# Four products of a pair summed in one PSUM bank, and fourteen more projections of the mixing stages computed as pairs

## The chip, the cores and the metric

The kernel runs on one core of one Trainium2 chip. The metric is the device time of one execution in microseconds. Every matmul works on float32 data split into a high and a low part (float32r), three matmuls for one product.

## The reference, cut to what matters

Two layers; each is an FFN, a mixing block with three branches, a second FFN and a gated embedding. All 544 tokens (512 of one prompt, 32 of eight samples) go through together. The mixing block is where most of the change lies:

```python
h = rmsnorm(x, w['g_mix'])
z = h @ w['w_in']
u_a, v_a, b_gate, c_gate, x_b, x_c, gates = jnp.split(z, SPLITS, axis=-1)
u_a = jax.nn.gelu(u_a)
v_a = layernorm(jax.nn.gelu(v_a), w['a_ln_g'], w['a_ln_b'])
y_a = chunk_spatial_gate(u_a, v_a, w['a_ws'], w['a_bs']) @ w['a_out']
conv_out, new_conv = short_conv(c_gate * x_b, conv_buf, w['b_conv'])
y_b = (b_gate * conv_out) @ w['b_out']
pooled, new_pool = multiscale_pool(x_c, pool_buf, start)     # windows 2, 4, 8, 16
y_c = (einsum(pooled, w['c_w']) * w['c_scale']) @ w['c_out']
g = jax.nn.sigmoid(gates)
x = x + (g[0] * y_a + g[1] * y_b + g[2] * y_c) @ w['w_o']
```

An FFN is `x + 0.5 * ((silu(gate) * up) @ w_down)` with `gate, up = split(rmsnorm(x) @ w_up)`.

## The kernel before

Activations stand with channels on the 128 partitions and the 544 tokens along the free axis, in slots of 128 x 544 float32 (85 slots in all, handed out in the order in which they came free). A weight block is 128 x 128; four blocks make a unit of 128 x 512, one DMA of 256 KB.

**Plain projections.** `gemm` (L302 is its matmul) multiplies one output block of 128 channels: 8 input blocks, three matmuls each, two halves of 272 tokens, so 48 matmuls of 272 columns, into a PSUM tile of two banks.

**Pairs.** `s_pair` computes two output blocks at once in the manner of Strassen and Winograd: seven products (`PRODUCTS`) of 12 matmuls of 272 columns each (L325 in `mm_s`), 84 matmuls where two plain projections have 96. Inputs B11, B21, B22 are halves of the input, T1 to T4 sums of halves; weights W12, W21, W22 are blocks, R1 to R4 sums of blocks. `ring_bank` hands out eight places of half a PSUM tile in turn; each product takes the next place, and ScalarE (L579) and VectorE (L581 to L593) add the seven results up in SBUF. FFN up-projections and the gates and U of the mixing block are pairs; C, XB, B and XC are plain; V is token-major (L807): tokens on the partitions, the normalized input as the stationary operand.

**Weights.** A planner lists all units in order. When TensorE's program reaches unit u, `unit` issues the low half of unit u+4 (L249, VectorE), the high half of u+5 (L244, ScalarE), the block sum of u+6 (L237, VectorE, for R3 and R4) and the loads of u+15 (SP's queue; for R1 and R2 a second load that accumulates, in POOL's queue). In plain stages `EXTRA` lets the low halves run up to 24 units ahead where slots allow.

**Order.** Every engine runs its instructions in program order, and the order is written out by hand. After each unit `tick` issues what is due: the `later` list (steps that follow a pair: SiLU, products, splits) and a share of the `background` list, such that it empties over a given number of ticks. `flush` issues all that is left at once.

**A mixing block**, in order: C0 and XB0 together, k outermost, with the rstd of the norm made beside them; then the background list of 24 steps that make the normalized input and the T sums of the pairs (`s_inputs` with `full`), over 24 ticks; convolution j (`conv_in`) after each of C/XB 1 to 3; V, its Gelu (L813) and its statistics (L814); B0 to B3; branch 1 (gate pairs and b_out); XC3 to XC0, each followed by its pooling (`pool_in`, `pool_mean`, `pool_out`); branch 2, where behind its first gate pair come the pool mixing (`c_mix`) and the first U pair; second U pair, spatial gate, branch 0, w_o.

Of the kernel before, what the change touches and what calls it, by code (L numbers as in the profile page):

```python
# [44 lines left out]
RMS_AT = 7, 14  # L45
RMS_AT0 = 8, 1
# [20 lines left out]
PRODUCTS = (("W21", "B11"), ("R3", "T2"), ("W22", "B21"), ("R1", "T1"), ("R2", "T3"), ("R4", "B22"), ("W12", "T4"))  # L67
# [35 lines left out]
class Kern:  # L103
# [217 lines left out]
    def mm_s(self, ps, w, xs, q, first, last):  # L321
        wh, wl = (a[:, q * P:(q + 1) * P] for a in w)
        xh, xl = xs
        for i, (a, b) in enumerate(((wl, xh), (wh, xh), (wh, xl))):
            self.nc.tensor.matmul(ps, a, b, start=first and i == 0, stop=last and i == 2)  # L325
# [77 lines left out]
    def s_inputs(self, gain, full):  # L403
# [5 lines left out]
        def steps(q):  # L409
# [45 lines left out]
            def sums():  # L455
                A, E = (e[0] for e in st["e"])
                st["t"] = self.slot()
                B = st["t"][0]
                nc.vector.tensor_sub(A[:, h1], A[:, h1], A[:, h2])
                nc.vector.tensor_sub(B[:, h2], A[:, h2], E[:, h2])  # L460
                nc.vector.tensor_add(B[:, h1], E[:, h2], A[:, h1])
                nc.vector.tensor_sub(A[:, h2], E[:, h1], B[:, h1])
                self.drop(st["e"][1])
# [103 lines left out]
    def s_pair(self, name, l, m1, m2, sets, s1, s2):  # L567
        nc = self.nc
        h1, h2 = slice(0, HT), slice(HT, T)
        q_ = self.slot()  # L570
        q1, V = q_[0][:, h1], q_[0][:, h2]
# [23 lines left out]
        self.drop(q_)  # L595

    def ff_group(self, up, l, j, inp, first, plain, hs, hsl):
# [47 lines left out]
        else:  # L645
            self.s_pair(up, l, NFF + j, j, inp.sets, o_, t_)
            d0()
# [59 lines left out]
    def to_seq(self, ps, buf, sbuf, lb, scale=True):  # L707
# [7 lines left out]
        for o, i, f in parts:  # L715
            if scale:
                nc.vector.tensor_mul(o, i, f)
            else:
                nc.scalar.activation(o, i, AF.Copy)
        return sv  # L720

    def mix(self, l, inp, nxt):
# [66 lines left out]
        assert len(xr) == KD  # L789
        self.drop(*xs)  # L790

# [6 lines left out]
        vslots = self.bank(3)  # L798
        vb = [vslots[i // 2][:, i % 2, :] for i in range(5)]
        self.extra = EXTRA[3]  # L800
        for k in range(KD):
            wh, wl = self.take("w_in", l, k, Z_V, 4)
            xh, xl = xr[k]
            for i in range(5):
                t0 = self.tok0(i)
                for q, (a, b) in enumerate(((xh, wl), (xh, wh), (xl, wh))):
                    nc.tensor.matmul(vb[i], a[:, t0:t0 + P], b, start=(k == 0 and q == 0), stop=(k == KD - 1 and q == 2))  # L807
# [4 lines left out]
        def v_in(i):  # L812
            nc.scalar.activation(vt[i][:, :SEQ], vb[i], AF.Gelu_apprx_tanh)  # L813
# [19 lines left out]

        for i in range(5):
            v_in(i)
        for j in range(G):
            pb, = self.gemm([W2(Z_B + j)])
            gate_b(j, pb)
# [433 lines left out]
```

## Time and profile before

| | us |
|---|---|
| median of 3 runs | 2437.67 (2436.99 to 2438.49) |
| span of the profiled execution, first to last instruction | 2435.3 |
| the rest of that median, outside the span | 2.4 |
| TensorE busy | 2414.3, 99% |
| VectorE busy | 1903.0, 78% |
| ScalarE busy | 1087.3, 45% |

The profile is of one execution. For that execution only the span is given; the times of the runs include what lies before the first and after the last instruction. A line such as L325 is a line of the kernel's file; a helper's line stands for all its callers. An entry "[2.50 <-PE ps L516]" says that the engine had stood idle for 2.50 us until TensorE's instruction of line 516 on tile ps was done.

### The profile page before, as it was taken

To read this page: it belongs to the slowest core of one execution; us is meant where nothing else is said; L and a number is where in the kernel's file an instruction comes from. 1 tells how busy PE (TensorE), PEld (TensorE's weight loads), DVE (VectorE), ACT (ScalarE), POOL (GpSimd) and SP (SyncE) were. 2 spreads that over 40 slices of the span, in tenths; PEclk is the share of its full clock that TensorE was granted. 3 is DMA by queue.
4 is the path that set the end of the run, shared out by engine and by line. 5 is a ranking of instruction groups with operands and counts; after the bars stand their busy time and mean duration, and the time that the engine had idled before them with its cause. 6 is when DMAs were issued, how large, how long until landed. Compare 5 with 4: busy or idle time off the path is not lost.

```text
span 2435.3 us, 48371 instructions
## 1 busy us (share of the span) xinstructions
PE 2414.3 (99%) x19016; PEld 2401.5 (99%) x19016; DVE 1903.0 (78%) x3583; ACT 1087.3 (45%) x2021; POOL 202.0 (8%) x248
## 2 busy tenths in 40 slices
PE   8999999999999999999999999999999999999997
PEld 8999999999999999999999999999999999999997
DVE  7887776778788887878788777866788779877775
ACT  6443444444446444435554444434354454434352
POOL 1111000010110100100010110000011011101000
PEclk9999999999999999999999999999999999999998
DMA  6665551354554555555255565523455536656521
GB/s 199 143 148 140 148 163 58 88 143 118 145 158 114 141 144 145 148 139 157 63 139 142 135 157 137 161 70 82 128 133 146 165 91 145 157 131 154 145 80 38
DMA packets 173988, 318.79 MB, mean 131 GB/s; under 512 B 19584, under 2 KB 21888, under 8 KB 173760
## 3 DMA queue, kind: packets, MB, share of 16 engines
q1 hardware_dynamic: 139248, 252.24, 34.2%
q0 software_dynamic: 32640, 61.16, 15.0%
q8 instruction: 149, 2.44, 0.4%
q10 hardware_dynamic: 1872, 2.29, 0.3%
q14 instruction: 79, 0.65, 0.1%
HBM read 312.63 MB, written 2.99 MB: 130 GB/s over the span
## 4 chain that ended last, share of the span: by engine, by line
PE 99%; DVE 0%; ACT 0%; DMA 0%; issue 0%; DVEq 0%; ACTq 0%
PE ps L325 47%; PE ps L302 46%; PE ps L807 2%; PE ps L1069 2%; PE ps L530 0%; PE ps L516 0%; PE ps L972 0%; DMA par<-in_par 0%; DVE s L1114 0%; PE ps L974 0%; DVE x L1096 0%; ACT s L1100 0%; ACT L502 0%; ACT L244 0%; DVE s L1095 0%
## 5 line engine op out<-in xcount | busy, mean ns | idle before, releaser
L325 PE MATMUL ps<-s,s 128*128 128x272 f32 x9156 | 1162.0, 288 | 0.0
L325 PEld LDWEIGHTS ps<-s,s 128*128 128x128 f32 x9156 | 1153.5, 188 | 0.4 <-DVE s L938 0.2
L302 PE MATMUL ps<-s,s 128*128 128x272 f32 x8880 | 1132.6, 288 | 7.3 <-ACT s L443 7.3
L302 PEld LDWEIGHTS ps<-s,s 128*128 128x128 f32 x8880 | 1121.7, 189 | 7.6 <-ACT s L443 7.2
L244 ACT ACTIVATE s<-s 128x512 fp32r<-128x512 f32 x1169 | 663.1, 621 | 506.0 <-DVE s L237 461.6
L249 DVE TENSOR_TENSOR s<-s,s 128x512 fp32r<-128x512 f32 x1169 | 768.3, 685 | 8.6 <-ACT s L244 8.6
L231 POOL DMA_DIRECT2D s<-in_wts x218 | 186.0, 854 | 1738.2 <-DMA s<-in_wts 448.5
L660 DVE SCALAR_TENSOR_TENSOR x<-ps,x 128x544 f32<-128x544 f32 x128 | 92.4, 722 | 137.2 <-PE ps L302 137.0
L579 ACT ACTIVATE s<-ps 128x272 f32<-128x272 f32 x109 | 43.2, 396 | 251.3 <-PE ps L325 251.1
L237 DVE TENSOR_TENSOR s<-s,s 128x512 f32<-128x512 f32 x218 | 149.3, 685 | 0.0
L581 DVE TENSOR_TENSOR s<-ps,s 128x272 f32<-128x272 f32 x109 | 48.0, 441 | 69.5 <-PE ps L325 43.3
L587 DVE TENSOR_TENSOR s<-ps,s 128x272 f32<-128x272 f32 x109 | 48.1, 441 | 63.8 <-PE ps L325 62.7
L607 ACT ACTIVATE s<-s 128x544 f32<-128x544 f32 x88 | 57.9, 658 | 89.4 <-DVE s L620 89.0
L613 ACT ACTIVATE s<-s 128x544 fp32r<-128x544 f32 x88 | 57.6, 654 | 59.8 <-DVE s L610 44.1
L864 DVE TENSOR_TENSOR s<-ps,s 128x544 f32<-128x544 f32 x48 | 34.8, 725 | 50.7 <-PE ps L302 46.2
L616 DVE TENSOR_TENSOR s<-s,s 128x544 fp32r<-128x544 f32 x88 | 63.2, 718 | 5.9 <-ACT s L613 5.8
L1069 PE MATMUL ps<-s,s 128*128 128x256 f32 (+1 forms) x480 | 61.6, 289 | 1.8 <-ACT rstd L532 1.8
L623 DVE TENSOR_TENSOR s<-s,rstd 128x544 f32<-128x544 f32 x88 | 63.2, 718 | 0.1
L1069 PEld LDWEIGHTS ps<-s,s 128*128 128x128 f32 x480 | 60.5, 188 | 2.0 <-ACT rstd L532 2.0
L610 DVE TENSOR_TENSOR s<-s,s 128x544 f32<-128x544 f32 x82 | 58.9, 718 | 0.4
L858 ACT ACTIVATE s<-s 128x544 f32<-128x544 f32 x48 | 29.0, 652 | 67.6 <-DVE s L593 67.6
L620 DVE TENSOR_TENSOR s<-s,rstd 128x544 f32<-128x544 f32 x82 | 59.0, 719 | 0.0
(133 smaller groups left out, 1176.4 us busy)
## 6 DMA issues: line engine op xcount, KB each, us to landing
s<-in_wts SPq DMA_DIRECT2D x951, 256.0 KB, 3.4
s<-in_wts POOLq DMA_DIRECT2D x218, 256.0 KB, 4.6
x<-in_xT ACTq DMA_DIRECT2D x4, 272.0 KB, 5.2
x<-in_xT SPq DMA_DIRECT2D x4, 272.0 KB, 4.8
s<-in_pT POOLq DMA_DIRECT2D x4, 272.0 KB, 3.2
out_yT<-s SPq DMA_DIRECT2D x4, 144.0 KB, 1.8
out_yT<-s ACTq DMA_DIRECT2D x4, 144.0 KB, 1.8
s<-in_st_in POOLq DMA_DIRECT2D x2, 272.0 KB, 3.1
```

Source lines behind the costliest of these rows:

```text
L231: self.nc.gpsimd.dma_start(out=t, in_=src(1 if w == "R1" else 2, 4), accum_op=ALU.add)
L237: self.nc.vector.tensor_add(self.new_raw(w, u0, 2 if w == "R3" else 1), self.read_raw(a, u0), self.read_raw(b, u0))
L244: self.nc.scalar.activation(a[0][:, :UC], self.read_raw(w, u0), AF.Copy)
L249: self.nc.vector.tensor_sub(lo, self.read_raw(w, u0), hi.bitcast(F32))
L302: self.nc.tensor.matmul(ps[:, h, :HT], a, bh, start=first and i == 0, stop=last and i == 2)
L325: self.nc.tensor.matmul(ps, a, b, start=first and i == 0, stop=last and i == 2)
L610: nc.vector.tensor_mul(o[:, :], o[:, :], t[:, :])
L616: nc.vector.tensor_sub(lo, o[:, :], hi.bitcast(F32))
L620: nc.vector.tensor_mul(t[:, :], t[:, :], self.rstd[:, :])
L623: nc.vector.tensor_mul(o[:, :], o[:, :], self.rstd[:, :])
L660: nc.vector.scalar_tensor_tensor(xm, self.pv(pst[i]), 0.5, xm, op0=ALU.mult, op1=ALU.add)
L1069: nc.tensor.matmul(ps, a, b[:, c], start=first and i == 0, stop=last and i == 2)
```

## The change

A pair takes four places of the ring, X, Y, Z and V, and skips one. The order of the products changes. R3, R1 and R4 go on accumulating in X on top of W21, with copies by ScalarE between them; the sign of T2 changes with it. The last evacuation can be given by the caller, so that rstd (FFN), the sigmoid (gates) or the Gelu (U) reads PSUM directly. In the mixing block V comes right after C0/XB0 and reads the input before normalization (rstd is then a scale of its Gelu, per token); the 24 input steps are spread over 9 ticks, the rest issued behind V; C/XB 1 to 3, B and XC become pairs, seven per layer. Pooling is cut into steps; the first U pair moves ahead of branch 2.

```diff
+V_TICKS = 9
-PRODUCTS = (("W21", "B11"), ("R3", "T2"), ("W22", "B21"), ("R1", "T1"), ("R2", "T3"), ("R4", "B22"), ("W12", "T4"))
+PRODUCTS = (("W21", "B11"), ("R2", "T3"), ("R3", "T2"), ("W22", "B21"), ("R1", "T1"), ("W12", "T4"), ("R4", "B22"))
...
+        X, Y, Z, V = (self.ring_bank()[:, :HT] for _ in range(4))
+        self.psi += 1
+        bank = {"W21": X, "R2": Y, "R3": X, "W22": Z, "R1": X, "W12": V, "R4": X}
         for i, (w, x) in enumerate(PRODUCTS):
-            bk = self.ring_bank()[:, :HT]
+            bk = bank[w]
             wt = self.s_unit(i, name, l, m1, m2)
+            new = w in ("W21", "R2", "W22", "W12")
             for q, xs in enumerate(sets):
-                self.mm_s(bk, wt, xs[x], q, q == 0, q == len(sets) - 1)
+                self.mm_s(bk, wt, xs[x], q, new and q == 0, q == len(sets) - 1, not new)
             if w == "W21":
-                nc.scalar.activation(q1, bk, AF.Copy)
+                nc.scalar.activation(b[:, h1], X, AF.Copy)
             elif w == "R3":
-                nc.vector.tensor_sub(V, bk, q1)
+                nc.scalar.activation(a[:, h2], X, AF.Copy)
+                nc.vector.tensor_sub(a[:, h1], Y, a[:, h2])
             elif w == "W22":
-                nc.vector.tensor_add(b[:, h1], bk, q1)
+                nc.vector.tensor_add(b[:, h1], Z, b[:, h1])
             elif w == "R1":
-                b5 = bk
-            elif w == "R2":
-                nc.vector.tensor_add(a[:, h1], bk, V)
-                nc.vector.tensor_sub(V, V, b5)
-                nc.vector.tensor_sub(a[:, h2], a[:, h1], b5)
+                nc.scalar.activation(b[:, h2], X, AF.Copy)
+                nc.vector.tensor_sub(a[:, h2], Y, b[:, h2])
+            elif w == "W12":
+                nc.vector.tensor_add(a[:, h1], V, a[:, h1])
             elif w == "R4":
-                nc.vector.tensor_sub(b[:, h2], bk, V)
-            else:
-                nc.vector.tensor_add(a[:, h1], a[:, h1], bk)
+                if last:
+                    last(b[:, h2], X)
+                else:
+                    nc.scalar.activation(b[:, h2], X, AF.Copy)
             self.tick()
...
         else:
-            self.s_pair(up, l, NFF + j, j, inp.sets, o_, t_)
-            d0()
+            r = self.rstd
+            self.s_pair(up, l, NFF + j, j, inp.sets, o_, t_,
+                        lambda out, ps: nc.vector.tensor_mul(out, ps, r[:, HT:]))
+            nc.vector.tensor_mul(t[:, :HT], t[:, :HT], r[:, :HT])
...
-        pc, px = self.gemm([W(Z_C), W(Z_XB)], kouter=True, hooks=self.rms_hooks(then=(steps, 24)))
+        pc, px = self.gemm([W(Z_C), W(Z_XB)], kouter=True, hooks=self.rms_hooks(then=(steps, V_TICKS)))
         conv_in(0, self.scaled(pc), conv_x(0, px))
-        for j in range(1, G):
-            pc1, = self.gemm([W(Z_C + j)])
-            c_ = self.scaled(pc1)
-            px1, = self.gemm([W(Z_XB + j)])
-            conv_in(j, c_, conv_x(j, px1))
...
-            nc.scalar.activation(vt[i][:, :SEQ], vb[i], AF.Gelu_apprx_tanh)
+            nc.scalar.activation(vt[i][:, :SEQ], vb[i], AF.Gelu_apprx_tanh, scale=self.cols[:, 16 + i:17 + i])
...
+        w = self.take("w_in", l, KD - 1, Z_V, 4)
         for i in range(5):
+            v_mm(KD - 1, w, i)
             v_in(i)
-        for j in range(G):
-            pb, = self.gemm([W2(Z_B + j)])
-            gate_b(j, pb)
+        while self.bg:
+            self.bg.popleft()()
+        self.drop(*xs)
+        for j in range(1, G):
+            c_, z_ = pair(Z_C + j, Z_XB + j)
+            conv_state(j)
+            conv_in(j, c_, self.slot(), z_)
+        for j in range(0, G, 2):
+            for i, b_ in enumerate(pair(Z_B + j, Z_B + j + 1)):
+                gate_b(j + i, b_)
...
-        for j in (3, 2, 1, 0):
-            st = {}
-            pj, = self.gemm([W2(Z_XC + j)])
-            pool_in(j, pj, st)
-            self.background([lambda j=j, st=st: pool_mean(j, st), lambda j=j, st=st: pool_out(j, st)], 3)
+        def pool_pair(j):
+            z1, z2 = pair(Z_XC + j, Z_XC + j + 1)
+            return pool_steps(j + 1, z2) + pool_steps(j, z1)
 
         self.flush()
+        self.background(pool_pair(2), 14)
+        fs = pool_pair(0)
+        self.flush()
+        self.background(fs, 12)
...
+        u_in(0)
 
         def c_mid():
+            self.flush()
             c_mix()
-            u_in(0)
```

`pool_steps` is a list: the input copies, one step per doubling of the window, the mean, and the split.

## Rows read from the trace of the kernel before

**Rows 1.** The page's first part: busy us (share of the span) xinstructions.

```profile
PE 2414.3 (99%) x19016; PEld 2401.5 (99%) x19016; DVE 1903.0 (78%) x3583; ACT 1087.3 (45%) x2021; POOL 202.0 (8%) x248
```

**Rows 2.** The chain that ended last, in order of time: start us, us, what.

```profile
433.12 27.75 PE ps L807 x120
460.87 24.05 PE ps L302 x192
484.91 10.52 PE ps L325 x84
```

**Rows 3.** Waits: engine, line, waited for, us in total, times, longest.

```profile
ACT s L579 <- PE ps L325: 251.1, 91, 5.5
...
PE ps L302 <- ACT s L443: 7.3, 1, 7.3
```

**Rows 4.** Groups by line: count, busy us, mean ns, idle before, releasers.

```profile
L249 DVE TENSOR_TENSOR s<-s,s 128x512 fp32r<-128x512 f32 x1169 | 768.3, 685 | 8.6 <-ACT s L244 8.6
L244 ACT ACTIVATE s<-s 128x512 fp32r<-128x512 f32 x1169 | 663.1, 621 | 506.0 <-DVE s L237 461.6 <-PE ps L302 31.7 <-PE ps L325 7.2
...
L587 DVE TENSOR_TENSOR s<-ps,s 128x272 f32<-128x272 f32 x109 | 48.1, 441 | 63.8 <-PE ps L325 62.7
...
L579 ACT ACTIVATE s<-ps 128x272 f32<-128x272 f32 x109 | 43.2, 396 | 251.3 <-PE ps L325 251.1
```

**Rows 5.** Timeline, first pair of an FFN: start us, us, instruction, count.

```profile
799.80 22.40 PE L325 MATMUL ps<-s,s 128*128 128x272 f32 x177
...
803.19 0.38 ACT L579 ACTIVATE s<-ps 128x272 f32<-128x272 f32 x1
```

**Rows 6.** Timeline, the pair behind the spatial gate.

```profile
671.01 10.77 PE L325 MATMUL ps<-s,s 128*128 128x272 f32 x84
...
674.04 0.38 ACT L579 ACTIVATE s<-ps 128x272 f32<-128x272 f32 x1
```

**Rows 7.** Timeline of VectorE behind V's statistics.

```profile
463.47 1.33 DVE L482 TENSOR_TENSOR s<-s,s 128x544 fp32r<-128x544 f32 x2
```

**Rows 8.** Timeline of VectorE and ScalarE at convolution 0 and during V.

```profile
397.87 0.69 DVE L748 TENSOR_TENSOR s<-s,s 128x512 f32<-128x512 f32 x1
...
399.44 0.31 ACT L760 ACTIVATE s<-cst,par 128x32 f32<-128x32 f32 x1
...
401.22 2.87 DVE L419 SCALAR_TENSOR_TENSOR s<-x,par,rstd 128x544 f32<-128x544 f32 x4
...
442.77 2.49 DVE L249 TENSOR_TENSOR s<-s,s 128x512 fp32r<-128x512 f32 x4
```

**Rows 9.** Timeline, pool 0 and the pair behind it.

```profile
574.95 10.67 PE L325 MATMUL ps<-s,s 128*128 128x272 f32 x84
575.15 0.76 ACT L719 ACTIVATE s<-ps 128x272 f32<-128x272 f32 x3 [1.64 <-PE ps L302]
...
575.84 0.71 DVE L907 TENSOR_TENSOR s<-s 128x526 f32<-128x526 f32 x1 [1.80 <-ACT s L719]
...
576.69 0.69 DVE L913 SCALAR_TENSOR_TENSOR s<-s,s 128x512 f32<-128x512 f32 x1
...
578.89 0.38 ACT L579 ACTIVATE s<-ps 128x272 f32<-128x272 f32 x1
```

**Rows 10.** Timeline of ScalarE at a change of its function table.

```profile
486.87 1.28 ACT L502 ACT_TABLE_LOAD   x1
488.17 0.21 ACT L502 ACTIVATE mv<-mv 128x5 f32<-128x5 f32 x1
```

**Rows 11.** Timeline, the pool mixing.

```profile
585.46 3.17 PE L302 MATMUL ps<-s,s 128*128 128x272 f32 x24
...
591.90 1.53 DVE L366 TENSOR_TENSOR s<-s,s 128x544 fp32r<-128x544 f32 x2
```

**Rows 12.** Stretches: busy us of PE, PEld, DVE, ACT, POOL; granted clock, DMA share, GB/s.

```profile
2400.00:2405.00 5.00, 3.24 (x25) 3.00 (x24) 3.64 (x9) 2.77 (x5) 0.00 (x0) 1.00 0.00 0
...
2420.00:2436.00 16.00, 3.29 (x15) 2.84 (x13) 7.42 (x23) 2.85 (x6) 0.00 (x0) 0.57 0.21 74
```

More of the change, by code (lines that the diff above doesn't have):

```diff
@@ L319, in gemm, with mm_s @@
         return pst
-    def mm_s(self, ps, w, xs, q, first, last):
+    def mm_s(self, ps, w, xs, q, first, last, go_on=False):
         wh, wl = (a[:, q * P:(q + 1) * P] for a in w)
@@ L324, in mm_s @@
         for i, (a, b) in enumerate(((wl, xh), (wh, xh), (wh, xl))):
-            self.nc.tensor.matmul(ps, a, b, start=first and i == 0, stop=last and i == 2)
+            self.nc.tensor.matmul(ps, a, b, start=first and i == 0, stop=last and i == 2, skip_group_check=go_on)
     def s_unit(self, i, name, l, m1, m2):
@@ L705, in nt, with to_seq @@
         return ap.rearrange("p (n t) -> p n t", t=t)
-    def to_seq(self, ps, buf, sbuf, lb, scale=True):
+    def to_seq(self, ps, buf, sbuf, lb):
         nc = self.nc
@@ L715, in to_seq @@
         for o, i, f in parts:
[L716 to L719, printed above, removed]
+            nc.vector.tensor_mul(o, i, f)
         return sv
@@ L797, in mix @@
         rows = [row("a_ln_g"), row("a_ln_b")]
-        vslots = self.bank(3)
+        vslots = [self.ps[(self.psi + i) % 4] for i in (0, 3, 1)]
+        self.psi += 2
         vb = [vslots[i // 2][:, i % 2, :] for i in range(5)]
         self.extra = EXTRA[3]
[L801 to L807, printed above, removed]
         vs = [self.slot() for _ in range(5)]
@@ L832, in v_bias, with v_mm @@
                 self.drop(rows[0], rows[1])
+        def v_mm(k, w, i):
+            wh, wl = w
+            xh, xl = xg[k]
+            t0 = self.tok0(i)
+            for q, (a, b) in enumerate(((xh, wl), (xh, wh), (xl, wh))):
+                nc.tensor.matmul(vb[i], a[:, t0:t0 + P], b, start=(k == 0 and q == 0), stop=(k == KD - 1 and q == 2))
+        for k in range(KD - 1):
+            w = self.take("w_in", l, k, Z_V, 4)
+            for i in range(5):
+                v_mm(k, w, i)
+        w = self.take("w_in", l, KD - 1, Z_V, 4)
         for i in range(5):
+            v_mm(KD - 1, w, i)
             v_in(i)
-        for j in range(G):
-            pb, = self.gemm([W2(Z_B + j)])
-            gate_b(j, pb)
+        while self.bg:
[3 more added lines that the diff above has]
+            c_, z_ = pair(Z_C + j, Z_XB + j)
+            conv_state(j)
+            conv_in(j, c_, self.slot(), z_)
+        for j in range(0, G, 2):
+            for i, b_ in enumerate(pair(Z_B + j, Z_B + j + 1)):
+                gate_b(j + i, b_)
         macc, merged, merged_s = [], [], []
@@ L855, in branch @@
             for m in range(0, KD, 2):
-                ts = pair(Z_G + br * KD + m, Z_G + br * KD + m + 1)
-                for t_ in ts:
-                    nc.scalar.activation(t_[0][:, :], t_[0][:, :], AF.Sigmoid)
+                ts = pair(Z_G + br * KD + m, Z_G + br * KD + m + 1, AF.Sigmoid)
                 if m == 0 and mid:
@@ L885, in mix, with pool_in @@
         po = st_po[0]
-        def pool_in(j, ps, st):
+        def pool_in(j, z_, st):
             st["sl"] = [self.slot() for _ in range(4)]
@@ L896, in pool_in, with pool_steps, begin, double @@
             nc.scalar.activation(self.nt(po[:, o:o + NS * LB], LB), sv[:, :, TS:], AF.Copy)
[L898 removed]
+        def pool_steps(j, z_):
             win = WINS[j]
[L900 to L906 removed]
+            st = {}
+            def begin():
+                pool_in(j, z_, st)
+                buf, ta, tb, sm = (t[0] for t in st["sl"])
+                st["cur"] = buf, sm[:, :QCOLS], 1
+                st["tmp"] = [(ta, sm[:, QCOLS:2 * QCOLS]), (tb, sm[:, 2 * QCOLS:3 * QCOLS])]
+            def double():
+                cur, scur, w = st["cur"]
+                nx, snx = st["tmp"][0]
+                st["tmp"].reverse()
@@ L915, in pool_mean @@
-            nc.vector.scalar_tensor_tensor(self.nt(out[:, SEQ:T], TS), cs[:, :, LB:], 1.0 / win,
-                                           st["sv"][:, :, LB:], op0=ALU.mult, op1=ALU.subtract)
-            h = win - 1
-            nc.vector.tensor_mul(out[:, :h], cur[:, LB:LB + h], self.par[:, PB_IC:PB_IC + h])
-            nc.vector.tensor_sub(out[:, :h], out[:, :h], buf[:, LB:LB + h])
-            st["o"] = next(t for t in st["sl"] if t[0] is out)
-            self.drop(*(t for t in st["sl"] if t is not st["o"]))
+                st["cur"] = nx, snx, 2 * w
@@ new lines, in mean @@
+            def mean():
+                cur, scur, _ = st["cur"]
+                buf, out = st["sl"][0][0], st["tmp"][0][0]
+                cs = self.nt(scur, LB + TS)
+                nc.vector.scalar_tensor_tensor(out[:, :SEQ], cur[:, LB:PCOLS], 1.0 / win, buf[:, LB:PCOLS],
+                                               op0=ALU.mult, op1=ALU.subtract)
+                nc.vector.scalar_tensor_tensor(self.nt(out[:, SEQ:T], TS), cs[:, :, LB:], 1.0 / win,
+                                               st["sv"][:, :, LB:], op0=ALU.mult, op1=ALU.subtract)
+                h = win - 1
+                nc.vector.tensor_mul(out[:, :h], cur[:, LB:LB + h], self.par[:, PB_IC:PB_IC + h])
+                nc.vector.tensor_sub(out[:, :h], out[:, :h], buf[:, LB:LB + h])
+                st["o"] = next(t for t in st["sl"] if t[0] is out)
+                self.drop(*(t for t in st["sl"] if t is not st["o"]))
@@ L923, in pool_out @@
+            return [begin] + [double] * (win.bit_length() - 1) + [mean, lambda: pool_out(j, st)]
         def pool_out(j, st):
```

67 lines of the change are left out of this document (27 added, 40 removed).

## The prediction

> **What bounds the kernel now.** I read the page's busy line first: TensorE is busy for 99% of the span, VectorE for 78, ScalarE for 45 [rows 1]. Then the chain in order of time, which is TensorE from end to end: a pair is 84 matmuls in 10.52 us, so a product 1.51, and a plain stretch of 192 matmuls takes 24.05 [rows 2]. Then the waits: TensorE's own view has four lines, the longest 7.3 us at the start (the others, 1.8 to 3.0 us, lie in the last stage) [rows 3]. Through all mixing and FFN stages TensorE waits for nothing. So a matmul taken away is time gained, a wait put in front of TensorE is time lost, both one for one, and the question is what waits the change makes.
>
> The groups by line give the other engines' prices [rows 4]: low half of a weight unit on VectorE 685 ns (L249; the weight sum, L237, is an addition of the same shape and taken alike), high half on ScalarE 621 (L244), a 272-column evacuation 396 on ScalarE (L579), 441 on VectorE (L587). Neighbours overlap: four L249 took 2.49 us, so they follow each other at (2.49 - 0.69)/3 = 0.60 us [rows 8]. With the same 0.085 off, I use 0.36 for short evacuations and 0.55 for a high half.
>
> **What goes.** Fourteen pairs replace 28 plain projections (per layer C/XB 1 to 3, two of B, two of XC). Two plain projections are 96 matmuls, half of 24.05; a pair saves 12.03 - 10.52 = 1.51 us [rows 2], fourteen **-21.1 us**. V keeps its 120 matmuls.
>
> **What comes: a deadline for ScalarE.** So far each product had a place of its own, read up to three products later. Now W21, R3, R1 and R4 add up in one place X, and TensorE may not start R3, R1 or R4 until ScalarE has copied X. One other product (R2, W22, W12) lies between, 1.51 us; a copy takes 0.40. So ScalarE may be about a microsecond late for nothing. It runs in order: ahead of a copy stand high halves, which wait for VectorE's sums, and background steps.
>
> *FFN pairs.* In 91 of 109 pairs ScalarE stood idle until W21 was done [rows 3], and VectorE gets less to do. For one back-to-back pair I count 9 weight operations at 0.60, 4 evacuations at 0.36, 0.7 for the rstd halves, 3 x 0.64 for the gate: 9.5 us of 10.5; the third copy, behind the sum for the next R3, ends 0.7 us early. Cost 0; with that cover gone, 0.1 us in each of 81 pairs is 8. The first pair of an FFN differs: its copy ran behind a flushed SiLU and split, 803.19 to 803.57; the pair began at 799.80, so R3 would be due at 802.81 [rows 5]. 0.76 late, three times: **+2.3**. Behind the spatial gate the copy ended at 674.42, R3 is due at 671.01 + 3.01 [rows 6]: 0.4, in two layers **+0.8**.
>
> *V to the first pair.* The 24 input steps go out over 9 ticks, but V has 8 units: 21 go out beside it, the last three (one high split, two low splits of T) stand in VectorE's queue behind V's five statistics. V's last matmul is at 433.12 + 27.75 = 460.87 [rows 2]; the statistics end at 463.47, two low splits take 1.33 [rows 7], the next two 1.27 more: done 5.2 us after V. The second product, R2 x T3, wants the last of them at 1.51 + 11/12 x 1.51 = 2.9. With a tenth of latency 2.4 us per layer, **+4.8**. Ahead of that VectorE has convolution 0 (4.8 with its evacuations) and 21 steps: 8 x 0.70 [rows 8], 12 x 0.64, 16 x 0.36, 19 us, against V's 27.75. So it reaches the statistics in time; some two us are left, and each weight half above three adds 0.6. Bounds per layer 1.5 to 5.
>
> *Pairs behind a convolution, three per layer.* Convolution j must now wait for ScalarE's copy of R4. In the old one VectorE was free 3.35 us after its first product (397.87 to 401.22), ScalarE 1.8 after it (399.44 + 0.31, less overlap) [rows 8]. From a pair's end: 0.5 + 1.8, a high half 0.55, the copy 0.4 = 3.25 against 3.01. VectorE, free at 3.85, makes a low half and a sum (5.05), ScalarE two high halves (6.2) and the next copy (6.6) against 6.3. 0.3 + 0.35 = 0.65 us, six times: **+3.9**. Bounds 0 to 8.
>
> *Pooling, the large one.* So far four plain projections of 6 us carried one pool each. Now pool 3 (four doublings) goes out in the second XC pair, and a flush sets all of pool 2 ahead of the next pair (U). The old kernel shows this in small, with pool 0 (one doubling) flushed ahead of a pair that began at 574.95: ScalarE's input copy at 575.15, a doubling at 575.84, the mean from 576.69, then split and high half, and the W21 copy from 578.89 to 579.27 [rows 9]. R3 would be due at 577.96: 1.31 late. Two things come on top. VectorE has in the second XC pair 8 x 0.60 + 4 x 0.36 + 4 x 0.85 + 1.1 up to pool 3's mean, and some 1.6 of waits for ScalarE: 12.3, so the mean ends 1.8 to 1.9 after the pair, its split takes 0.55, and pool 2's copy starts 2.25 later than pool 0's. And pool 2 has two doublings more, 1.7. 1.31 + 2.25 + 1.7 = 5.2 us per layer, **+10.4**. Bounds 3 (VectorE on time) to 7.
>
> Pools 1 and 0 then run beside that U pair and the gate pair behind it. U's third copy is 0.4 late. At U's end ScalarE has pool 1's split, a high half, the Gelu table (1.28 [rows 10]), three Gelus (1.35), a high half and the copy: if the table starts 1.1 after the pair, the copy ends at 4.75 against 3.0, 1.75 late. The gate pair's third copy 0.35. 2.5 us per layer, **+5.0**; bounds 0 to 4 each.
>
> The Trainium skill (ScalarE: Activation LUTs, section What ACT_TABLE_LOAD costs) counts a drain of some 1.38 us with each load. The trace disagrees: the load began at 486.87 and the Sqrt behind it at 488.17 [rows 10]. By the page's figure the sum would be 2 to 3 us higher.
>
> *Pool mixing.* U's first pair lay between the pool mixing and the first c_out projection and now stands ahead of both. The mixing began at 585.46 on TensorE, its last low half ended at 593.43, 7.97 later [rows 11]. c_out now follows at 3.01, wants that half for its last two matmuls, and ends at 8.2 in place of 6.0. 2.0 per layer, **+4.0**; bounds 0 to 2.5.
>
> *At no cost.* A pair has 7 weight loads for 4, on SP and POOL; FFNs run four pairs in a row without a TensorE wait [rows 3]. The layer-norm rows pass ahead of V in POOL's queue; the accumulating loads behind them are wanted 15 units later. If that cover is gone, a product waits for a landing; rival 1's 16 us is far above that. V's scale rides on its Gelu.
>
> **Sum.** 2.3 + 0.8 + 4.8 + 3.9 + 10.4 + 5.0 + 4.0 = 31.2 us of waits less 21.1: +10.1. The profiled execution spans 2435.3; the median of the runs, 2437.67, is 2.4 above it, which I take as time around the span, unchanged. 2435.3 + 10.1 + 2.4 = 2447.8: **2448 us**, 0.4% slower.
>
> **Rivals.** (1) *The covers hold; faster.* Only places where the old trace has a late copy pay, at the old size: 3.1, the U pair 2 x 1.3, the mixing 2 x 2.0: 9.7 in all, 2437.7 - 21.1 + 9.7 = 2426. For it: the 91 copies that waited for TensorE, and VectorE's 78%. Against it: the flush, and the queue behind the statistics. It decides at the U pair's first copy, up to 1.3 late, and it stays faster until waits reach 16 us. (2) *Only pooling pays*: 10.4 + 4.0 + 3.1 = 17.5, 2434, too little to tell. For it: the margins elsewhere are tenths of a us. Against it: the three steps behind the statistics. (3) *The clock falls in the new holes.* Once TensorE runs dry at the end the granted clock of the stretch is 0.57, while a hole of 1.8 us at 2400 left it at 1.00 [rows 12]; a 5 us hole lies between. At the lower level (1.2 GHz) the 60 matmuls left of a U pair would cost 7.5 us more; half of that in two layers makes 2456. The Trainium skill (TensorE: Matmul & The Clock Gate, Part 1) says that an idle array falls to half rate until it has been busy again; the tail agrees, and no run here shows a 5 us hole.
>
> **Chances.** Forecast 0.47 (own range 2442 to 2457), rival 1 0.28, rival 2 0.16, rival 3 0.09. A measurement of this kernel tells 0.2%, 4.9 us, from no change. Faster is rival 1 but for its upper edge, 0.27; the same is rival 2 and the edges of its neighbours, 0.2; slower 0.53. The bounds of the terms add up to 12 and 56 us of waits, 2429 to 2473; all at the upper end together is unlikely, and rival 1 reaches 2426. Range 2425 to 2459.
>
> **What would show it.** About 2393 us of matmuls and some 30 of TensorE waits, nearly all for ScalarE's copies of X: one hole of 5 us per layer before the third product of the first U pair; 2.4 in the second product behind V; 2 in the first c_out; 0.3 and 0.35 in pairs behind a convolution; 0.8 in an FFN's first pair, none in its others. It is wrong if the U pair's hole is under 2 us, if FFN pairs in a run take over 10.6 each, or if the pairs behind V run at 10.5.

## The result, and the profile after

The changed kernel takes 2452.8 us (median; 2452.5 to 2453.3), the kernel before on the same chip 2437.3: ratio 1.0064, 95% interval 1.0049 to 1.0078. It is slower, by 15.5 us. 2448 was forecast, with a range of 2425 to 2459. The span of the profiled execution is 2451.1 us, 15.8 above the 2435.3 of before.

The page's busy line answers to [rows 1]; its columns are the same.

```profile
PE 2407.8 (98%) x18848; PEld 2386.7 (97%) x18848; DVE 1861.8 (76%) x3439; ACT 1215.0 (50%) x2357; POOL 226.3 (9%) x276
```

TensorE has 168 matmuls fewer (14 pairs in place of 28 plain projections, 12 fewer each), but its busy time fell by 6.5 us and not by 21.1: a stretch at a lower clock (below) and the end of a matmul ahead of a wait count as busy too. VectorE has less to do in the whole kernel; where it has more comes in the experiments.

TensorE's waits answer to [rows 3]; the columns are the waiting tile and line, the releaser, us in total, times and the longest. Lines have moved by a few places: L326 is a pair's matmul, L303 a plain one, L833 one of V.

```profile
PE ps L326 <- ACT s L582: 14.6, 13, 5.2
PE ps L303 <- ACT s L444: 7.0, 1, 7.0
PE ps L833 <- ACT s L807: 3.1, 4, 0.8
...
PE ps L326 <- DVE s L483: 2.4, 4, 0.6
...
PE ps L303 <- DVE s L367: 1.2, 4, 0.3
PE ps L326 <- ACT s L584: 0.3, 2, 0.2
```

The view had four lines before; the one of 7.0 is the old start. What is new is ScalarE's copy of X (L582), V's Gelu (L807), the late low halves of the pair inputs (L483) and of the pool mixing (L367). TensorE's timeline shows where they lie in the first layer's mixing stage and at the head of its second FFN (start us, us, instruction, count, and in brackets the wait ahead of it):

```profile
422.45 1.66 PE L833 MATMUL ps<-s,s 128*128 128x512 f32 x6 [0.78 <-ACT s L807]
424.89 1.66 PE L833 MATMUL ps<-s,s 128*128 128x512 f32 x6 [0.78 <-ACT s L807]
...
429.62 0.64 PE L326 MATMUL ps<-s,s 128*128 128x272 f32 x3 [0.56 <-DVE s L483]
430.89 1.28 PE L326 MATMUL ps<-s,s 128*128 128x272 f32 x8 [0.63 <-DVE s L483]
...
442.06 3.28 PE L326 MATMUL ps<-s,s 128*128 128x272 f32 x24 [0.19 <-ACT s L582]
445.49 7.81 PE L326 MATMUL ps<-s,s 128*128 128x272 f32 x60 [0.16 <-ACT s L584]
...
579.25 13.58 PE L326 MATMUL ps<-s,s 128*128 128x272 f32 x84 [5.22 <-ACT s L582]
593.37 7.80 PE L326 MATMUL ps<-s,s 128*128 128x272 f32 x60 [0.54 <-ACT s L582]
...
606.11 1.01 PE L303 MATMUL ps<-s,s 128*128 128x272 f32 x6 [0.31 <-DVE s L367]
...
810.43 5.78 PE L326 MATMUL ps<-s,s 128*128 128x272 f32 x44 [0.65 <-ACT s L582]
```

The 84 matmuls from 579.25 took 13.58 us, where 84 took 10.52 before [rows 2]. The table of stretches says why (busy us of PE, PEld, DVE, ACT and POOL with their counts, the granted clock, DMA share, GB/s):

```profile
573.00:579.00 6.00, 1.03 (x9) 0.81 (x7) 5.25 (x14) 2.98 (x9) 0.00 (x0) 0.97 0.04 7
579.00:586.00 7.00, 6.75 (x31) 6.75 (x32) 6.61 (x15) 4.09 (x11) 0.86 (x1) 0.54 0.57 181
```

Right behind the hole the granted clock is 0.54 and 31 matmuls fill 6.75 us; at 0.125 each (10.52 / 84) 54 would have. That is 23 x 0.125 = 2.9 us in this layer. The second layer has the same hole, but fewer of its matmuls fall into the low stretch:

```profile
1789.00:1797.00 8.00, 7.91 (x46) 7.91 (x47) 7.23 (x16) 4.84 (x13) 1.63 (x2) 0.70 0.65 193
```

At 0.125 each 63 matmuls would have filled these 7.91 us; 17 are missing, 2.2 us.

What set the 5.2 us stands in ScalarE's timeline, which answers to [rows 9]:

```profile
572.88 0.66 ACT L362 ACTIVATE s<-s 128x544 fp32r<-128x544 f32 x1 [1.43 <-DVE s L940]
573.45 0.61 ACT L903 ACTIVATE s<-s 128x512 f32<-128x512 f32 x1
...
577.74 0.66 ACT L362 ACTIVATE s<-s 128x544 fp32r<-128x544 f32 x1 [3.02 <-DVE s L940]
578.30 0.61 ACT L245 ACTIVATE s<-s 128x512 fp32r<-128x512 f32 x1
578.82 0.38 ACT L582 ACTIVATE s<-ps 128x272 f32<-128x272 f32 x1
```

The copy of X (L582) stands behind pool 2's input copy (L903), three doublings and a mean on VectorE (3.02 us of waiting for L940), a split and a high half: the steps of the forecast.

### The profile page after: what moved, and what is told of

Read it like the earlier page. It is cut to its first block, busy times and chain, and to the rows that moved or that the text cites. A ratio compares the mean times of both kernels' runs of the same rounds, so it can differ in the third digit from the quotient of the medians.

```text
span 2451.1 us, 48091 instructions
## 1 busy us (share of the span) xinstructions
PE 2407.8 (98%) x18848; PEld 2386.7 (97%) x18848; DVE 1861.8 (76%) x3439; ACT 1215.0 (50%) x2357; POOL 226.3 (9%) x276
## 4 chain that ended last, share of the span: by engine, by line
PE 93%; DVE 3%; ACT 3%; issue 1%; DMA 0%; DVEq 0%; ACTq 0%
PE ps L326 49%; PE ps L303 38%; PE ps L1094 2%; PE ps L833 2%; ACT s L245 1%; PE ps L531 0%; PE ps L517 0%; DVE s L926 0%; DVE s L250 0%; DVE s L1006 0%; ACT s L807 0%; ACT s L362 0%; DVE s L483 0%; ACT L738 0%; DVE s L238 0%
## 5 line engine op out<-in xcount | busy, mean ns | idle before, releaser
L326 PE MATMUL ps<-s,s 128*128 128x272 f32 x10332 | 1321.2, 289 | 18.2 <-ACT s L582 14.6
L326 PEld LDWEIGHTS ps<-s,s 128*128 128x128 f32 x10332 | 1307.7, 189 | 24.1 <-ACT s L582 18.4
L303 PE MATMUL ps<-s,s 128*128 128x272 f32 x7536 | 965.1, 288 | 8.2 <-ACT s L444 7.0
L303 PEld LDWEIGHTS ps<-s,s 128*128 128x128 f32 x7536 | 953.0, 189 | 9.8 <-ACT s L444 6.9
L250 DVE TENSOR_TENSOR s<-s,s 128x512 fp32r<-128x512 f32 x1211 | 812.5, 686 | 21.8 <-ACT s L245 19.9
L245 ACT ACTIVATE s<-s 128x512 fp32r<-128x512 f32 x1211 | 702.6, 623 | 230.8 <-DVE s L238 225.8
L232 POOL DMA_DIRECT2D s<-in_wts x246 | 210.7, 875 | 1941.4 <-DMA s<-in_wts 761.7
L582 ACT ACTIVATE s<-ps 128x272 f32<-128x272 f32 x123 | 48.7, 396 | 468.9 <-PE ps L326 468.9
L238 DVE TENSOR_TENSOR s<-s,s 128x512 f32<-128x512 f32 x246 | 168.7, 686 | 0.0
L585 DVE TENSOR_TENSOR s<-ps,s 128x272 f32<-128x272 f32 x123 | 54.3, 442 | 113.8 <-ACT s L584 112.3
L584 ACT ACTIVATE s<-ps 128x272 f32<-128x272 f32 x123 | 48.8, 397 | 103.6 <-PE ps L326 102.2
L590 DVE TENSOR_TENSOR s<-ps,s 128x272 f32<-128x272 f32 x123 | 54.3, 442 | 56.6 <-ACT s L589 55.8
L589 ACT ACTIVATE s<-ps 128x272 f32<-128x272 f32 x123 | 48.7, 396 | 92.1 <-PE ps L326 92.0
L616 ACT ACTIVATE s<-s 128x544 fp32r<-128x544 f32 x88 | 57.9, 658 | 37.1 <-DVE s L613 21.1
L610 ACT ACTIVATE s<-s 128x544 f32<-128x544 f32 x88 | 57.9, 658 | 19.6 <-DVE s L652 18.0
L626 DVE TENSOR_TENSOR s<-s,rstd 128x544 f32<-128x544 f32 x88 | 63.5, 722 | 0.1
L833 PE MATMUL ps<-s,s 128*128 128x512 f32 x240 | 56.9, 395 | 3.1 <-ACT s L807 3.1
```

Source lines behind the costliest of these rows:

```text
L232: self.nc.gpsimd.dma_start(out=t, in_=src(1 if w == "R1" else 2, 4), accum_op=ALU.add)
L238: self.nc.vector.tensor_add(self.new_raw(w, u0, 2 if w == "R3" else 1), self.read_raw(a, u0), self.read_raw(b, u0))
L245: self.nc.scalar.activation(a[0][:, :UC], self.read_raw(w, u0), AF.Copy)
L250: self.nc.vector.tensor_sub(lo, self.read_raw(w, u0), hi.bitcast(F32))
L303: self.nc.tensor.matmul(ps[:, h, :HT], a, bh, start=first and i == 0, stop=last and i == 2)
L610: nc.scalar.activation(t[:, :], t[:, :], AF.Silu)
```

## Where the 15.8 us came from

A hole is measured here from the start of the last matmul ahead of it to that of the next, less the usual 0.126 (0.231 between two matmuls of V, 27.75 / 120 in [rows 2]); it is 0.1 to 0.3 us longer than the wait.

| term of the prediction | forecast | measured |
|---|---|---|
| fourteen pairs | -21.1 | 168 matmuls fewer, -21.1 |
| first pairs of an FFN, 3 | 2.3 | 0.81 + 0.81 + 0.80 = 2.4 |
| behind the spatial gate, 2 | 0.8 | 0.27 + 0.28 = 0.55 |
| V to the first pair, 2 layers | 4.8 | 2 x (0.72 + 0.79) = 3.0 |
| behind a convolution, 6 | 3.9 | 6 x (0.34 + 0.31) = 3.9 |
| first copy in the U pair, 2 | 10.4 | 2 x 5.38 = 10.8 |
| U's third copy and the gate pair, 2 | 5.0 | 2 x (0 + 0.70) = 1.4 |
| c_out behind the pool mixing, 2 | 4.0 | 2 x (0.47 + 0.47) = 1.9 |
| not forecast: V's own matmuls, 4 | 0 | 4 x 0.95 = 3.8 |
| first pair of the first FFN | 0 | 0.3 |
| clock behind the U pair's hole, 2 | 0 | 2.9 + 2.2 = 5.1 |
| not forecast: the second matmul behind each of the 32 other holes | 0 | 32 x 0.11 = 3.4 |

The last row is read from the start times of the matmuls in the trace: behind a hole the second matmul starts some 0.11 us later than the usual spacing has it. The measured holes are 24.0 us of the 31.2 forecast and 4.1 that were not; with 5.1 of clock and 3.4 behind the holes, less 21.1, that is 15.5 of the 15.8.

## The experiments

The theory to start with: TensorE loses what ScalarE's copies of X come late, and each hole has the mechanism of its term. The rival, which grew out of the first results: VectorE's amount of work in the mixing stages, whatever empties the banks.

**V's last block in another order.** The five token tiles lie two to a PSUM tile: 0 and 1, 2 and 3, 4 alone.

```diff
-        for i in range(5):
+        for i in (0, 2, 4, 1, 3):
             v_mm(KD - 1, w, i)
             v_in(i)
```

> The changed kernel with one line else: the last input block of V is multiplied in the token order 0, 2, 4, 1, 3. Theory (V's new waits come from its Gelus: banks 0 and 1, and 2 and 3, are halves of one PSUM tile, and the matmuls into one half wait until ScalarE has read the other): the four waits of 0.78 us in V go, the statistics end 1.8 us earlier per layer, and so does the second product behind V: 2452.8 - 3.6 = 2449. Rival (the end of the T splits is set by VectorE's steps, not by the Gelus): the waits move into the first pair and the time stays within 1 us of 2452.8.

Measured: 2448.7 us, ratio 1.0050 (1.0033 to 1.0066). The four waits of 0.78 are gone; the first pair's first wait grew from 0.56 to 0.84 (timeline of TensorE):

```profile
423.80 2.68 PE L326 MATMUL ps<-s,s 128*128 128x272 f32 x20
427.32 0.65 PE L326 MATMUL ps<-s,s 128*128 128x272 f32 x3 [0.84 <-DVE s L483]
```

So the matmuls of token tile 1 waited until the Gelu had read tile 0: another bank, but the same tile.

**The hole filled.** Idle matmuls go into place V, which no product needs yet, behind R2 of the first U pair, to keep TensorE running through the hole.

```diff
+            if w == "R2":
+                for _ in range(fill):
+                    nc.tensor.matmul(V, wt[0][:, :P], sets[0]["B11"][0], start=True, stop=True)
             self.tick()
...
+us.extend(pair(Z_U + j, Z_U + j + 1, AF.Gelu_apprx_tanh, 0 if j else 40))
```

> The changed kernel with 40 idle matmuls (5.0 us at the full rate, results unused and overwritten) into place V behind product R2 of the first U pair, where TensorE has its hole of 5.2 us. It adds work and takes no wait away. Theory (the hole lets TensorE's clock fall to its lower level for 6.8 us per layer, worth 3.4 us each): the hole is filled, R3 starts when it did, the granted clock stays at 1.00, 2452.8 - 6.8 = 2446. Rival (the slow stretch behind the hole has another cause, weights or memory): 2453 or more, clock as before.

Measured: 2451.1 us, ratio 1.0057 (1.0042 to 1.0072). Timeline of TensorE (L600 is the filling), then the stretch:

```profile
574.06 5.22 PE L600 MATMUL ps<-s,s 128*128 128x272 f32 x40
...
586.00 4.78 PE L326 MATMUL ps<-s,s 128*128 128x272 f32 x36 [0.26 <-ACT s L589]
592.06 7.77 PE L326 MATMUL ps<-s,s 128*128 128x272 f32 x60 [1.28 <-ACT s L582]
```

```profile
574.00:589.00 15.00, 14.58 (x114) 14.14 (x112) 14.52 (x35) 8.47 (x23) 1.73 (x2) 1.00 0.40 113
```

The clock stayed at 1.00: the hole was what let it fall. But only 1.7 us came back (2.8 between the two profiled executions) where 6.8 were expected. The low clock had cost 5.1 and not 6.8, and new waits take part of that: R4 now waits 0.26 and the gate pair's first copy 1.28 for 0.54, in each layer. VectorE is busy for 14.52 of the 15 us: it was behind there too, and the low clock had covered part of it.

**No flush ahead of the U pair.** Pools 2, 1 and 0 go out as one list.

```diff
-        fs = pool_pair(0)
-        self.flush()
-        self.background(fs, 12)
+        self.background(pool_pair(0), 14)
```

> The changed kernel without the flush between the second XC pair and the first U pair: the steps left of pools 3 and 2 and those of 1 and 0 go out in one list over 14 ticks, beside the U pair and the gate pair. Theory (the flush puts pool 2 ahead of ScalarE's copy of X): the hole of 5.2 us per layer falls to under 2, the clock stays, some 3 us per layer come back as small waits: 2452.8 - 6.8 - 5 = 2441. Rival (VectorE has too much to do in these three pairs wherever it stands): the 5 us are spread over the two pairs, only the clock's 6.8 is won: 2446.

Measured: 2463.5 us, ratio 1.0109 (1.0094 to 1.0124); the expected gain turned into a loss. The U pair's first copy is on time, and the waits come behind it:

```profile
574.14 6.32 PE L326 MATMUL ps<-s,s 128*128 128x272 f32 x48 [0.36 <-ACT s L582]
581.53 4.78 PE L326 MATMUL ps<-s,s 128*128 128x272 f32 x36 [1.07 <-ACT s L589]
588.23 9.32 PE L326 MATMUL ps<-s,s 128*128 128x272 f32 x60 [1.91 <-ACT s L582]
598.97 0.77 PE L303 MATMUL ps<-s,s 128*128 128x272 f32 x4 [1.43 <-ACT s L362]
...
608.36 4.83 PE L303 MATMUL ps<-s,s 128*128 128x272 f32 x23 [5.46 <-ACT s L362]
```

The last one is of another kind. VectorE's timeline has

```profile
606.84 1.48 DVE L961 TENSOR_SCALAR s<-ps,par 128x544 f32<-128x544 f32 x2 [6.16 <-DMA out_po<-s]
```

With the pools living longer the slots ran short: a tile of the pool mixing got the slot of the pooling state, whose output DMA had just been issued.

**The same, and that slot kept until the pool mixing is done.**

```diff
-                self.drop(st_po, st_in)
+                self.drop(st_in)
...
             c_mix()
+            self.drop(st_po)
```

> The kernel without the flush ahead of the first U pair (2463.5), and the tile of the pooling state kept until the pool mixing is done, so that no tile of the mixing takes its place. Theory (VectorE's scaling of the pool mixing stood 6.16 us behind the state's output DMA, since its tile had taken the place of the state just sent): that wait goes, and the 5.5 to 6.1 us hole in front of the first c_out product of each layer with it, and at least half of the low clock behind it: 2463.5 - 11.6 - 4 = 2448 (2444 to 2451). Rival (VectorE is that far behind by its own work, the DMA only ended last): 2458 to 2463.

Measured: 2448.7 us, ratio 1.0050 (1.0035 to 1.0065), as the theory had it; VectorE's wait is gone. The waits in front of it (1.10, 1.92 and 1.43) are as they were: 0.36 + 1.10 + 1.92 + 1.43 are 4.8 us a layer, so without the flush most of the 5.2 is spread, not saved. VectorE has almost no idle time there: from 565 to 590 us it is busy for 24.72 of 25 us, and from 575 on the stretch reads

```profile
575.00:606.00 31.00, 25.64 (x182) 24.33 (x181) 28.66 (x62) 21.57 (x47) 3.97 (x5) 0.94 0.53 145
```

The kernel is 4.1 us below the changed one, and its clock is low in one short stretch of the first layer alone (0.57 from 588 to 592, right behind the wait of 1.92).

**The sum alone.** The kernel before, its mixing stages untouched, with the change's `s_pair` and T sums.

```diff
+        X, Y, Z, V = (self.ring_bank()[:, :HT] for _ in range(4))
+        self.psi += 1
+        bank = {"W21": X, "R2": Y, "R3": X, "W22": Z, "R1": X, "W12": V, "R4": X}
...
-            bk = self.ring_bank()[:, :HT]
+            bk = bank[w]
```

> The kernel before with one part of the change alone: the pairs sum four products in one place (new order of products, signs, ring, FFN evacuation); the mixing stages stay as they were. Theory (the summing saves TensorE nothing and makes it wait wherever ScalarE's copy is late): first FFN pairs 3 x 0.8, spatial 2 x 0.3, the pairs behind the last pool and behind the pool mixing 2 x 1.3 and 2 x 1.8: 9.2 us, 2437.3 + 9.2 = 2446. Rival (three evacuations fewer per pair let VectorE come in time there too): 2437 to 2440.

Measured: 2446.0 us, ratio 1.0036 (1.0023 to 1.0049). Two of its holes, behind pool 0 and behind the pool mixing:

```profile
579.13 7.78 PE L325 MATMUL ps<-s,s 128*128 128x272 f32 x60 [1.19 <-ACT s L581]
...
593.82 6.40 PE L325 MATMUL ps<-s,s 128*128 128x272 f32 x49 [0.90 <-ACT s L581]
```

The four-product sum alone costs 8.6 us; 8.2 are holes ahead of ScalarE's copies (2.4 in the FFN, 4.8 in these two over both layers, 0.7 behind the spatial gate, 0.3 in the first pair).

**The mixing alone.** The change's mixing stages with the pairs of before, so that ScalarE has no deadline.

```diff
-            bk = bank[w]
+            bk = self.ring_bank()[:, :HT]
...
-                nc.scalar.activation(a[:, h2], X, AF.Copy)
-                nc.vector.tensor_sub(a[:, h1], Y, a[:, h2])
+                nc.vector.tensor_sub(V, bk, q1)
```

> The changed kernel with the pairs of before: seven products into seven places of the ring, all evacuated by VectorE, the mixing stages as in the change. Theory (the deadline that ScalarE's copies of X set, 9 to 14 us after a place's product instead of the length of a ring, is what turns each late neighbour into a hole): the holes in front of second and third products go (5.2 us in the first U pair, 0.8 in the FFN's first pairs, 0.5 in the gate pair), the V tile's 0.78 waits and what is late behind V stay, so 2437 - 21 + 6 for V and its first pair + 4 for what comes behind the convolutions and the pool mixing + 2 for a smaller pool hole = 2428 (2424 to 2433). Rival (the stretch from V to the c_out product is bound by VectorE's own work, whoever empties the banks): the hole moves to the pool mixing and the c_out product and the time is 2438 or more.

Measured: 2458.2 us, ratio 1.0091 (1.0074 to 1.0107). My theory falls here: the new pairs without the sum are no faster, but slower still. Waits and stretch:

```profile
582.97 6.27 PE L326 MATMUL ps<-s,s 128*128 128x272 f32 x36 [3.72 <-DVE s L901]
...
601.38 0.74 PE L303 MATMUL ps<-s,s 128*128 128x272 f32 x4 [1.13 <-DVE s L590]
603.47 6.46 PE L303 MATMUL ps<-s,s 128*128 128x272 f32 x36 [1.35 <-DVE s L367]
```

```profile
575.00:606.00 31.00, 24.59 (x171) 23.76 (x171) 29.82 (x72) 19.81 (x44) 3.12 (x4) 0.91 0.45 128
```

VectorE is busy for 29.8 of 31 us while TensorE idles. TensorE waits ahead of the pooling too: 0.38, 1.12 and 1.94 us in B and branch 1. The same time in the kernel before, and in the changed one (the work in it differs: before, it holds pool 0, a gate pair, the pool mixing and U's first pair; with the change, pools 2, 1 and 0 beside U's and the gate pair, then the pool mixing):

```profile
575.00:606.00 31.00, 31.00 (x248) 30.84 (x248) 28.48 (x54) 18.45 (x36) 3.98 (x5) 1.00 0.60 154
```

```profile
575.00:606.00 31.00, 26.01 (x178) 25.29 (x178) 27.93 (x62) 21.40 (x45) 4.01 (x5) 0.89 0.57 151
```

Before, VectorE was at 92% there with TensorE never waiting: 2.5 us of room, while the page says 78% for the kernel. A pair takes 1.51 us from TensorE. It gives VectorE three low halves more (7 units for 4; 1211 in the changed kernel, 1169 before) and two block sums (246 and 218), 0.69 us each, and four to seven evacuations. VectorE's busy total is 1805.5 us with the sum alone and 1861.8 in the changed kernel: with all that hangs on them, fourteen pairs put 4.0 us each on VectorE.

**The pooling's doublings left out.** This is the kernel without the flush and with the slot kept.

```diff
-                nx, snx = st["tmp"][0]
...
-                st["cur"] = nx, snx, 2 * w
+                st["cur"] = cur, scur, 2 * w
```

> The kernel without the flush and with the state's tile kept (2448.7), and with the pooling's doublings left out (20 of VectorE's additions, 10 us of its work a layer; the means are then of wrong sums): steps and their ticks stay. Theory (VectorE's amount of work between the pooling's pairs and the c_out product is what the holes of 0.5, 1.3, 2.1, 1.6 and 0.5 us there are made of): they go, all but 1 us a layer, and the time is 2448.7 - 2 x 5.5 = 2438 (2435 to 2441). Rival (ScalarE's copies come late by their place in its queue, VectorE's amount doesn't matter): the holes keep over 4 us a layer, 2445 or more.

Measured: 2439.7 us, ratio 1.0013 (1.0004 to 1.0022): 9.0 us less than with them. U's pair runs without a wait:

```profile
565.77 18.90 PE L326 MATMUL ps<-s,s 128*128 128x272 f32 x149
585.42 7.79 PE L326 MATMUL ps<-s,s 128*128 128x272 f32 x60 [0.76 <-ACT s L582]
594.24 4.85 PE L303 MATMUL ps<-s,s 128*128 128x272 f32 x34 [1.03 <-ACT s L362]
```

Of the waits of 0.36, 1.10, 1.92 and 1.43 a layer 0.76 and 1.03 are left, and VectorE has room again (20.66 of 25 us from 565 to 590):

```profile
575.00:606.00 31.00, 28.62 (x219) 27.50 (x219) 26.83 (x55) 21.75 (x46) 3.97 (x5) 1.00 0.55 146
```

So TensorE's loss around the pooling goes with VectorE's work, though the waits are booked on ScalarE, which stands behind VectorE. The doublings also lie in the chain that ScalarE's splits wait for, so this run alone does not tell the amount of VectorE's work from the length of that chain; that VectorE was busy without a break with them speaks for the amount.

**All 24 steps ahead of the statistics.**

```diff
-V_TICKS = 9
+V_TICKS = 8
```

> The changed kernel with V_TICKS 8 for 9: all 24 steps of the pair inputs are issued before V's statistics. Theory (the first pair behind V waits for three last steps that stand behind the statistics on VectorE): its two waits (0.56 and 0.63 us, twice) go, V's Gelus stay as they are, 2452.8 - 2.4 = 2450.4 (2449.5 to 2451.5). Rival (the steps' own pace, not their place behind the statistics): the waits stay within 0.2 us and the time is 2452.8.

Measured: 2455.0 us, ratio 1.0074 (1.0059 to 1.0089): neither theory; 2.3 slower than the changed kernel. The first pair's waits went, as my theory said, but ScalarE's timeline shows what I had not counted:

```profile
420.36 1.21 ACT L478 ACTIVATE s<-s 128x544 fp32r<-128x544 f32 x2 [1.90 <-DVE s L483]
421.58 1.28 ACT L807 ACT_TABLE_LOAD   x1
422.88 0.69 ACT L807 ACTIVATE s<-ps,cols 128x512 f32<-128x512 f32 x1
```

The last high splits wait for VectorE and now stand ahead of V's first Gelu, and with them its table load. V's matmuls of token tile 1 wait 2.30 us for that Gelu instead of 0.78, and the clock is low behind it (0.51 from 424 to 431). In the order 0, 2, 4, 1, 3 the Gelu has most of that time: in the next run V waits 1.2 us, once a layer.

**The mixing alone, with both edits of V.** The edits are those above, on the kernel with seven places.

```diff
-V_TICKS = 9
+V_TICKS = 8
...
+        for i in (0, 2, 4, 1, 3):
```

> The kernel with the change's mixing and the pairs of before, with the last V block in the token order 0, 2, 4, 1, 3 and V_TICKS 8. Theory (holes add up): 2428 for the seven places, less 3 for V's tile waits and 2 for the first pairs behind V: 2423 (2419 to 2428), faster than both kernels. Rival (VectorE bounds the stretch): within 1 us of the kernel with seven places alone, 2438 or more.

Measured: 2453.6 us, ratio 1.0068 (1.0053 to 1.0083). Neither theory gave this time: 2423 is far off, and the rival had it within 1 us of the 2458.2. Against 2458.2 on the same chip the two edits gain 4.7 us together, near the 5 that the sum of holes gave (the runs of the two kernels spread over 6.0 and 3.2 us), but from a base that VectorE bounds: the holes of 3.9, 1.3 and 1.5 around the pooling did not move.

**Two forms in one kernel.** The sum and ScalarE's copies only where VectorE has no room (C, XB, B and the gate pairs of branch 1, right behind B), the seven places elsewhere; XC plain and its order as before; V early with both edits. Ten of the fourteen new pairs stay. The T sums are those of the change, so `s_pair7` is the old function with the sign of R3's product turned.

```diff
+            if four:
+                self.s_pair("w_in", l, z1, z2, sets, s1, s2, ...)
+            else:
+                self.s_pair7("w_in", l, z1, z2, sets, s1, s2)
...
+            pj, = self.gemm([("w_in", l, Z_XC + j, xr, 0)])
```

> Both forms of the pair in one kernel: the four-product sum, emptied by ScalarE, only in the ten new pairs of C, XB and B and in the gate pairs of the second branch; the seven places of before in the FFN, in U and in the other gate pairs; XC, pooling, pool mixing and U in the order of before, XC plain; V early, its last block in the order 0, 2, 4, 1, 3, with V_TICKS 8. Theory (each form costs only where its own engine is late: the sum where ScalarE's copy is behind other copies, the seven places and the pooling's pairs where VectorE has no room): 2437.0 - 10 pairs at 1.51 + 1.2 behind V in each layer + 0.67 behind each of six convolutions = 2428 (2424 to 2433), faster than before. Rival (ten pairs fill VectorE so far that the backlog reaches the pooling, whatever the form): the holes come back between 480 and 610 us and the time is 2436 or more.

Measured: 2429.8 us (2429.7 to 2430.2), ratio 0.9970 (0.9959 to 0.9981): faster than both kernels, 7.1 us below the one before. Its waits (the other lines are the start and the last stage), and the stretch from 575:

```profile
PE ps L871 <- ACT s L845: 1.7, 2, 0.8
PE ps L327 <- ACT s L613: 1.1, 6, 0.2
PE ps L327 <- ACT s L615: 0.5, 3, 0.2
```

```profile
575.00:606.00 31.00, 31.00 (x248) 30.90 (x247) 28.61 (x53) 18.10 (x32) 3.41 (x4) 1.00 0.62 171
```

TensorE is full again there. Ten pairs are 15.1 us, the holes 2 x 1.0 and 12 of about 0.33, 6.0 in all, and the second matmuls behind them 14 x 0.11 = 1.5: 7.6 of gain, 7.1 measured. XC, the pooling and U stand here as in the kernel before, so no run tells whether XC's pairs or the later pools had filled VectorE; XC as pairs with earlier pooling was not tried.

**The seven places behind the convolutions too.**

```diff
-            c_, z_ = pair(Z_C + j, Z_XB + j)
+            c_, z_ = pair(Z_C + j, Z_XB + j, None, False)
```

> The kernel with two forms (2429.8), with the seven places in the six pairs of C and XB too: the sum emptied by ScalarE stays in the pairs of B and the gate pairs behind them alone. Theory (behind a convolution ScalarE's copies are late and VectorE still has room, as its backlog can be worked off in B's pairs): the waits of 0.2 us ahead of the second and third product of each of the six go and nothing comes instead, 2429.8 - 6 x 0.4 = 2427.4 (2426.5 to 2428.5). Rival (VectorE's backlog from the six pairs reaches B's pairs and the second branch, where the kernel with seven places alone had holes of 0.5, 1.3 and 2.1 us a layer): 2431 or more.

Measured: 2430.6 us, ratio 0.9973 (0.9962 to 0.9983), not to be told from the kernel with two forms and between what the two theories expected. The small waits went, V's wait grew from 0.8 to 1.2 us, and a new one came in the first of B's pairs:

```profile
463.42 3.27 PE L327 MATMUL ps<-s,s 128*128 128x272 f32 x24 [1.32 <-ACT s L613]
```

## Why the prediction was right, point by point

*The bound.* TensorE's time was the measure: 168 matmuls went, and each wait put in front of it was lost. The two terms worked out most closely hold within 0.4 us: the flush ahead of the first U pair (5.2 a layer forecast, a wait of 5.22) and the pairs behind a convolution (0.3 + 0.35, measured 0.34 + 0.31). The FFN's first pairs hold too (0.76, measured 0.81), and the other FFN pairs have no wait, as forecast.

*Terms that were mis-sized.* V to the first pair: 2.4 a layer, measured 1.5, the same three late steps. (The room ahead of the statistics is 27.75 - 4.8 - 19 = 3.9 us by the prediction's own terms, not some two; it did not enter the 2.4.) U's third copy and the gate pair: 2.5 a layer, measured 0.7; U's third copy was not late, and I took a gate copy 1.75 late, it was 0.54. c_out: 2.0 a layer (8.2 less 6.0 is 2.2), measured 0.9. For the gate copy the run with the hole filled shows why it came out small: at the low clock TensorE itself was late, and the wait rose from 0.54 to 1.28 once it was not. For c_out it does not: its two waits stayed at 0.31. There the last low half ended 7.3 us after the mixing began, not 7.97.

*What was missed.* V's own matmuls wait for the Gelu of the neighbour in their PSUM tile; I had costed V's move by its first pair alone. The run with another order gained 4.1 us. The matmuls behind each hole that start late (3.4 us) were not in the sum either.

*The clock.* Rival 3 had the mechanism, at a chance of 0.09: behind each 5.2 us hole the clock was low, 5.1 us gross against the 7.5 it gave. It should have been a term of the forecast. What it costs in the end is less, 1.7 us by the run with the hole filled (2.8 between the profiled executions). The Trainium skill (TensorE: Matmul & The Clock Gate, Part 1) says that an idle array falls to half rate until it has been busy again; the 0.54 behind the hole (1 is 2.4 GHz, 0.5 is 1.2) agrees, and so does 1.00 with the hole filled.

*What the prediction put down to the wrong owner.* It called the deadline of ScalarE's copies what the change brings and gave VectorE's 78% as a reason for rival 1. The sum alone, the mixing alone and the run without doublings show two causes. The sum's deadline costs 8.6 us where the pairs of before were free. And around the pooling VectorE, 92% busy there before, falls behind in either form of the pairs; how much of that is the pairs' own work and how much the later pools is open. Rival 1 (the covers hold) fails there; rival 2 (only pooling pays) had the largest place right but not its size, and left out V and the convolutions.

*Luck.* That the sum came within 5 us of the time is luck in part: the forecast waits were 7.2 us too high, and 12.6 us (holes that were not forecast, the clock, the late matmuls behind the holes) stood nowhere in it.

## What to carry to other kernels

A matmul scheme that saves TensorE time hands work per saved us to the engine that prepares and empties its tiles (here 4.0 us of VectorE for 1.51 of TensorE); read that engine's busy share in the stretch where the scheme goes (here 28.5 of 31 us), not in the whole kernel (78%). A wait is booked on the last releaser: ScalarE's late copies were VectorE's backlog, and taking away a queue order (the flush) only moved them, while taking away work removed most of them, and leaving out XC's pairs, with the pools early again, all. The form of a tile's evacuation can be chosen by place: sums in one bank where VectorE is full, places of their own where ScalarE's queue is late. The kernel with two forms was built so and is 7.1 us faster than before; that each place has its best form is not shown, and behind the convolutions the form made no difference.

## What was not expected of the hardware

The granted clock fell behind holes shorter than the 5.2 us one too: with all steps ahead of the statistics the stretch from 424 to 431 had 0.51, right behind a wait of 2.30 among V's last blocks, and with the slot kept the stretch from 588 to 592 had 0.57 behind a wait of 1.92. The second layer of that kernel kept 1.00 behind a wait of 1.95 (1794 to 1800), and the kernel without doublings, with waits up to 1.0 us in its layers, kept it everywhere in them. The table load showed no drain here either: it began at 421.58, took 1.28, and the Gelu began at 422.88, as in [rows 10].
